# A hybrid decoder layer in float32 on one core: the low halves of the feed-forward weights made by an accumulating DMA

## Chip, core and metric

One core of one Trainium2 chip runs the whole layer in one launch. The metric is the time of one execution on the device in microseconds (us), median of several runs.

## What is computed

One decoder layer on 512 tokens of width 1024, in float32: a first feed-forward, a mixer (a state-space group and differential attention side by side, one projection out), and a second feed-forward. Only the feed-forwards are touched; each is, with d_ff = 2816:

```python
def swiglu(h, w_gate, w_up, w_down):
    return (jax.nn.silu(h @ w_gate) * (h @ w_up)) @ w_down

x = x + 0.5 * swiglu(rms_norm(x, ffn1_norm_w[l]), ffn1_w_gate[l], ffn1_w_up[l], ffn1_w_down[l])
...
x = x + 0.5 * swiglu(rms_norm(x, ffn2_norm_w[l]), ffn2_w_gate[l], ffn2_w_up[l], ffn2_w_down[l])
```

## The kernel before

**Three products for one.** To keep float32's accuracy on TensorE (PE) in its faster float32r type, each operand is split into a high half, its value rounded to float32r, and a low half, the rest. A product is then hi x hi + hi x lo + lo x hi: three matmuls into one bank of PSUM (`mm3`, lines 168 to 172, and `product`, lines 322 to 328).

**Weights come in pieces.** `load_raw` (line 119) loads a piece of up to 128 x 1024 from HBM on SP's queue into one of three `raw` buffers. `split_part` (line 124) makes the halves: the high one by a copy on ScalarE (ACT) into `whi` (at the start of the program and in attention, `pool_hi`, on GpSimd, POOL), the low one by a subtraction on VectorE (DVE) into `wlo`:

```python
    def split_part(raw, hi, lo, a, b):
        if pool_hi[0]:
            G.tensor_scalar(hi[:, a:b], raw[:, a:b], 1.0, 1.0, op0=ALU.mult, op1=ALU.mult)
        else:
            S.copy(hi[:, a:b], raw[:, a:b])
        V.tensor_sub(lo[:, a:b], raw[:, a:b], hi[:, a:b].bitcast(F32))
```

`whi` and `wlo` have four buffers each, which go round: a piece's halves can be written only when PE has read the piece four places before it. The list `pieces` (line 113) holds all pieces of the layer in the order of their use; `prep` (line 139) prepares them in that order, `piece(ahead)` (line 159) hands out the next and prepares one or two further ones.

**A feed-forward** has 22 column tiles for gate and up, in four parts of six or four tiles. Its work is of three kinds (`ffn_plan`, line 73):

- The first part's gate and up take plain pieces of 1024 columns, 24 matmuls of 512 columns each (`std`, line 367; 12 pieces in the first feed-forward, 8 in the second).
- The other parts' gate and up go in pairs of tiles, in a form of Strassen's product with seven block products in place of eight (`seven`, line 330). A *seven* needs two loaded pieces, r1 and r2. Four subtractions on DVE (lines 152 to 155) make a scratch `tw` of two pieces from them. Then there are four splits (line 156), called s0 to s3 here: r1, the first and the second half of `tw`, and half of r2 (512 columns). Each of s0 to s2 serves two block products, s3 one; a block product is 12 matmuls of 256 columns, so a seven is 84. There are 16 sevens in the first feed-forward and 18 in the second.
- The products with w_down (`down`, line 354) take one piece per 128 rows of x: 768 columns (or 512, in parts of four tiles) and three matmuls of 512 columns for each tile. Eight downs of a part run one or two at a time behind the next part's sevens; the last part's eight end the feed-forward. A down ends with an update of x on DVE (line 362).

After the last downs of the first feed-forward, `done1` (line 415) copies x to DRAM on POOL's DMA queue (`xsave`, line 419) and prepares the mixer's operands `xhm`, `xlm` (lines 236, 237) and sums of squares (line 247, on POOL).

**Order.** The program is written in the order above; the framework then sets each engine's order by a list schedule of its own. An engine takes its instructions in its order and stands at one whose semaphores are not there yet.

Of the kernel before, what the change touches and what calls it, by code (L numbers as in the profile page):

```python
# [8 lines left out]
F32 = mybir.dt.float32  # L9
# [4 lines left out]
ALU = mybir.AluOpType  # L14
AX = mybir.AxisListType.X
PSUM = bass.MemoryType.PSUM
DRAM = bass.MemoryType.DRAM

P = 128
T = 512  # L20
# [18 lines left out]
def hymba_layer(ctx: ExitStack, tc: tile.TileContext, xT, gu1, dn1, wxbc, wdt, wz, wv, wqk,  # L39
                wo, gu2, dn2, cols, rows, out):  # L40
    nc = tc.nc
    V, S, G, PE = nc.vector, nc.scalar, nc.gpsimd, nc.tensor
# [4 lines left out]
    psum = {}  # L47

    def psum_open(**bufs):
        """One set of PSUM pools at a time: A tiles take two banks, M and J tiles one."""  # L50
        for cm, _ in reversed(list(psum.values())):
            cm.__exit__(None, None, None)
        psum.clear()
        for tag, n in bufs.items():
            cm = tc.tile_pool(name=f"ps{tag}", bufs=n, space=PSUM)
            psum[tag] = (cm, cm.__enter__())
# [14 lines left out]
        return psum["P"][1].tile([P, T], F32, tag="P", name=name)  # L71

    def ffn_plan(parts, early):
        """Order of the work: a part's products with w_down run between the next part's with gate and up."""
        plan, downs, f = [], [], 0
        for pi, n in enumerate(parts):
            if pi == 0:
                plan += [("std", e, g) for e in range(n) for g in range(2)]
            else:
                for c in range(n):  # L80
                    if pi == 1 and c == 0:
                        plan += downs[:early]
                        downs = downs[early:]
                    plan.append(("seven", f + c // 2 * 2, c % 2))
                    while downs and len(downs) > KD * (n - 1 - c) // n:
                        plan.append(downs.pop(0))
            downs = [("down", pi, d) for d in range(KD)]
            f += n
        return plan + downs
# [23 lines left out]
    pieces = ffn_pieces(gu1, dn1, PARTS1, EARLY1) + [("plain",) + p for p in mixp] + ffn_pieces(gu2, dn2, PARTS2, EARLY2)  # L113
    ready = []
    taken = [0]
    scratch = {}
    pool_hi = [False]

    def load_raw(src, n):
        raw = wpool.tile([P, 1024], F32, tag="raw", name="raw", bufs=3)  # L120
# [3 lines left out]
    def split_part(raw, hi, lo, a, b):  # L124
        if pool_hi[0]:
            G.tensor_scalar(hi[:, a:b], raw[:, a:b], 1.0, 1.0, op0=ALU.mult, op1=ALU.mult)  # L126
        else:
            S.copy(hi[:, a:b], raw[:, a:b])  # L128
        V.tensor_sub(lo[:, a:b], raw[:, a:b], hi[:, a:b].bitcast(F32))  # L129

    def hi_lo():
        return wpool.tile([P, 1024], F32R, tag="whi", name="whi"), wpool.tile([P, 1024], F32R, tag="wlo", name="wlo")
# [41 lines left out]
    xpool_cm = tc.tile_pool(name="x1", bufs=1, side="right")  # L174
    xpool = xpool_cm.__enter__()
    x1 = [xpool.tile([P, T], F32, name=f"x1_{d}") for d in range(KD)]
    # products of zeros while the first loads run: the tensor engine's clock is up when the data comes
    zeros = const.tile([P, T], BF16, name="zeros")
    V.memset(zeros, 0.0)
    warm = pP("warm")  # L180
# [24 lines left out]
    xnpool = xn_cm.__enter__()  # L205

    def rsqrt(dst, v, shape, tag):
        """dst = v ** -0.5 for small tiles: exponent-halving start and Newton steps."""
        y = tiny.tile(shape, F32, tag=f"rs_y{tag}", name="rs_y")
        t = tiny.tile(shape, F32, tag=f"rs_t{tag}", name="rs_t")  # L210
        ti = t.bitcast(I32)
        V.tensor_scalar(ti, v.bitcast(I32), 1, None, op0=ALU.arith_shift_right)
        V.tensor_scalar(y.bitcast(I32), ti, -1, 0x5F3759DF, op0=ALU.mult, op1=ALU.add)
        for it in range(3):
            V.tensor_mul(t, y, y)
            V.scalar_tensor_tensor(t, t, -0.5, v, op0=ALU.mult, op1=ALU.mult)
            V.scalar_tensor_tensor(dst if it == 2 else y, t, 1.5, y, op0=ALU.add, op1=ALU.mult)

    class Normed:
        """x * w in two parts, and the factors 1/rms(x) by token (columns, and a row on all partitions)."""  # L220

        def __init__(self, pool, sqp, wcol, name):
            self.sqp, self.pool = sqp, pool
# [46 lines left out]
    first = []  # L270
# [4 lines left out]
    for d in range(KD):  # L275
# [6 lines left out]
                split_part(first[i], *ready[i], sl.start, sl.stop)  # L282
        n1.square(d, x1[d])
    pool_hi[0] = False
    prep(4)

    def ffn(xn, x, done, name, parts, early):
        """x += 0.5 * swiglu(xn).

        The 128-column tiles of gate and up in the first part take the products as they are. The others take them in  # L290
        pairs, in Winograd's form of Strassen's product of 2x2 blocks (halves of the contraction, of the tokens
        and the two tiles), seven block products in place of eight, on the normalized tokens.
        """
        sp_cm = tc.tile_pool(name=f"str{name}", bufs=1)
        hp_cm = tc.tile_pool(name=f"ffn{name}", bufs=5)
        sp, hp = sp_cm.__enter__(), hp_cm.__enter__()
# [1 line left out]
        al = sp.tile([P, 4, 7, 256], F32R, name=f"al{name}")  # L298

        def operands(i):  # L300
            # 0: A12, 1: A22, 2: S1, 3: S2, 4: S3, 5: S4, 6: A11, 7: A21
            tx = hp.tile([P, 8, 256], F32, tag="hp", name="tx")
            for k, at in ((i, 6), (i + 4, 0)):
                c = xn.wcol + k
                V.scalar_tensor_tensor(tx[:, at:at + 2, :].rearrange("p a b -> p (a b)"), x[k], col[:, c:c + 1],
                                       xn.rbc, op0=ALU.mult, op1=ALU.mult)
            V.tensor_add(tx[:, 2], tx[:, 7], tx[:, 1])
            V.tensor_sub(tx[:, 3], tx[:, 2], tx[:, 6])
            V.tensor_sub(tx[:, 4], tx[:, 6], tx[:, 7])
            V.tensor_sub(tx[:, 5], tx[:, 0], tx[:, 3])  # L310
            S.copy(ah[:, i], tx[:, 0:7])
            V.tensor_sub(al[:, i], tx[:, 0:7], ah[:, i].bitcast(F32))

        def h_pair(g, u):
            """silu(g) * u in two parts; g and u: the two tiles, [P, 2, T]."""
            h = hp.tile([P, 2, 2, T], F32R, tag="hp", name="h")
            S.activation(g, g, AF.Silu)
            V.tensor_mul(u, u, g)
            S.copy(h[:, 0], u)
            V.tensor_sub(h[:, 1], u, h[:, 0].bitcast(F32))  # L320
            return h
# [6 lines left out]
                PE.matmul(ps, lhsT=lo, rhs=ah[:, i, a], start=False, stop=i == 3)  # L328

        def seven(c, u, nm_):  # L330
            """c[:, f, t] = the pair's two tiles by the two halves of the tokens."""
            w = piece(1)
            q = [pP(f"{nm_}{z}") for z in range(4)]
            half = lambda z, b: q[z][:, b * 256:(b + 1) * 256]
            cc = c.rearrange("p f (t b) -> p f t b", t=2)
            c1, u2, u3, u4 = (u[:, z] for z in range(4))
            product(half(0, 0), 6, w[0], 0)
            product(half(0, 1), 0, w[0], 512)
            S.copy(c1, half(0, 0))
            V.tensor_add(cc[:, 0, 0], half(0, 1), c1)  # L340
            product(half(1, 0), 2, w[1], 0)
            product(half(1, 1), 4, w[1], 512)
            product(half(2, 0), 3, w[2], 0)
            V.tensor_add(u2, half(2, 0), c1)
            V.tensor_add(u3, half(1, 1), u2)
            V.tensor_add(cc[:, 1, 1], half(1, 0), u3)
            V.tensor_add(u4, half(1, 0), u2)
            product(half(2, 1), 1, w[2], 512)
            V.scalar_tensor_tensor(cc[:, 0, 1], half(2, 1), -1.0, u3, op0=ALU.mult, op1=ALU.add)
            product(half(3, 0), 5, w[3], 0)  # L350
            V.tensor_add(cc[:, 1, 0], half(3, 0), u4)
# [56 lines left out]
        hp_cm.__exit__(None, None, None)  # L408
        sp_cm.__exit__(None, None, None)

# [1 line left out]
    xsave = dram.tile([KD, P, T], F32, name="xsave")  # L412
    nm = [None]

# [4 lines left out]
        G.dma_start(xsave[d], x1[d])  # L419

    ffn(n1, x1, done1, "1", PARTS1, EARLY1)
    nm = nm[0]
    xpool_cm.__exit__(None, None, None)
    psum_open(A=2, M=2, J=2)

# [1 line left out]
    mix_cm = tc.tile_pool(name="mix", bufs=1)  # L427
    mix = mix_cm.__enter__()
    row = mix.tile([P, NROW], F32, name="row")
# [134 lines left out]
    for n, pair in enumerate(order):  # L564
# [4 lines left out]
        for i in range(2):  # L569
            w = piece()  # L570
# [17 lines left out]
    V.tensor_scalar(e2, nm.v, EPS, None, op0=ALU.mult)  # L588

    def tok_proj(name, cb, ahead=2):  # L590
        """Projection onto 256 columns by token blocks; yields after each block's matmuls."""
        ws = [piece(ahead), piece(ahead)]
        for half in range(2):
            ps = pJ(f"{name}_{half}")
            psv = ps.rearrange("p (b c) -> p b c", c=256)
            for jj in range(2):
                j = half * 2 + jj
                o = psv[:, jj, :]
                for k in range(KD):
                    w = ws[k // 4]  # L600
# [129 lines left out]
            pass  # L730
    last_ssd = lambda: drain_c(8)

# [1 line left out]
    def rsqrt_act(dst, v, shape):  # L734
        """dst = v ** -0.5: exp(-ln(v) / 2) and a Newton step."""
        y = tiny.tile(shape, F32, tag="ra_y", name="ra_y")
        t = tiny.tile(shape, F32, tag="ra_t", name="ra_t")
        S.activation(y, v, AF.Ln)
        S.activation(y, y, AF.Exp, scale=-0.5)
        V.tensor_mul(t, y, y)  # L740
        V.scalar_tensor_tensor(t, t, -0.5, v, op0=ALU.mult, op1=ALU.mult)
        V.scalar_tensor_tensor(dst, t, 1.5, y, op0=ALU.add, op1=ALU.mult)
# [124 lines left out]
        G.tensor_scalar(v, v, -0.5, 1.5, op0=ALU.mult, op1=ALU.add)  # L867
        G.tensor_mul(o, o, v)

    # output projection pieces that fill the tensor engine while the last head's attention runs  # L870
    yhl = []

    def y_split():
# [141 lines left out]
    xn_cm.__exit__(None, None, None)  # L1015
    psum_open(P=8)

# [1 line left out]
    def done2(d):  # L1019
        nc.sync.dma_start(out[d], x2[d])  # L1020

    ffn(n2, x2, done2, "2", PARTS2, EARLY2)


# [59 lines left out]
```

## Times and profile before

| | |
|---|---|
| time, median of 3 runs (lowest to highest) | 1205.1 us (1204.64 to 1206.91) |
| span of the profiled execution, first to last instruction | 1203.1 us, 2.0 us under that median |
| busy: PE, DVE, ACT, POOL | 1163.4, 926.0, 533.8, 210.6 us |
| DMA: loads and stores on SP's queue; POOL's queue | 114.15 MB; 4.20 MB |
| first feed-forward, by its products | 6 to 357 us |
| second, by its products | 854 us to the end |

How to read it: a busy share is an average over stages with different limits, so what a change in one stage is worth is read in a table of that stage's stretches. PE's matmuls overlap in the records (the mean "duration" of one is longer than the distance between two), so the pace is read from the chain of work, which lists the distance. The clock is the share of TensorE's full clock that was granted: 1.00 is 2.4 GHz, 0.50 is 1.2 GHz. The DMA share is the mean busy share of the core's 16 DMA engines.

### The profile page before, as it was taken

The page shows a single profiled execution, that of the slowest core. Times are in us where ns is not written, and L with a number is a line of the kernel's source. Part 1 is how long each engine was busy: PE and PEld are TensorE (multiplying, and loading weights), DVE is VectorE, ACT ScalarE, POOL GpSimd, SP SyncE. Part 2 cuts the span into 40 slices and gives each one's busy share as a digit, 9 for nine tenths or more (in the row PEclk, how much of TensorE's full clock was granted, in tenths as well). Part 3 has the DMA queues.
Part 4 walks back from the last instruction along what each step waited for, and adds up shares of the span by engine and source line. Part 5 has one row for each costly group of instructions (what it writes and reads, how often), then busy time and mean ns, then how long its engine had stood idle before and what let it go on. Part 6 is the DMA issues. An engine that isn't in the chain of part 4 may idle for free.

```text
span 1203.1 us, 19035 instructions
## 1 busy us (share of the span) xinstructions
PE 1163.4 (97%) x7483; PEld 1036.3 (86%) x7483; DVE 926.0 (77%) x1593; ACT 533.8 (44%) x863; POOL 210.6 (18%) x214
## 2 busy tenths in 40 slices
PE   8999999999989999798999998899999999999998
PEld 6889999999967788797998886688789999999997
DVE  6988787787585867989588989636499988787862
ACT  5534343433352355343366675735244443434331
POOL 1000000000031004443255756315100000000000
PEclk9999999999998999899999999999999999999999
DMA  7223333333353224242321102216312333333332
GB/s 231 86 75 97 110 110 97 99 107 88 97 193 114 77 82 140 81 131 73 105 71 36 58 32 76 75 44 209 98 62 89 109 121 100 101 107 102 96 114 83
DMA packets 42393, 119.56 MB, mean 99 GB/s; under 512 B 4608, under 2 KB 9920, under 8 KB 42304
## 3 DMA queue, kind: packets, MB, share of 16 engines
q1 hardware_dynamic: 41024, 114.15, 30.3%
q0 software_dynamic: 1280, 4.20, 1.0%
q8 instruction: 59, 0.97, 0.3%
q14 instruction: 30, 0.25, 0.1%
HBM read 112.00 MB, written 6.32 MB: 98 GB/s over the span
## 4 chain that ended last, share of the span: by engine, by line
PE 40%; DVE 10%; issue 2%; ACT 2%; POOL 1%; DMA 0%; DVEq 0%; ACTq 0%; POOLq 0%
PE s L327 5%; PE s L326 5%; PE s L328 5%; PE dn L170 3%; PE dn L172 3%; PE dn L171 3%; PE wo L170 2%; PE wo L171 2%; PE wo L172 2%; DVE nmx L813 2%; DVE pe L823 1%; PE gu L170 1%; PE gu L172 1%; PE gu L171 1%; DVE wlo L129 1%
## 5 line engine op out<-in xcount | busy, mean ns | idle before, releaser
L129 DVE TENSOR_TENSOR wlo<-raw,whi 128x1024 fp32r<-128x1024 f32 (+3 forms) x225 | 225.9, 1007 | 120.0 <-ACT whi L128 104.4
L128 ACT CAST whi<-raw 128x1024 fp32r<-128x1024 f32 (+2 forms) x204 | 175.7, 865 | 310.2 <-PE s L327 121.7
L327 PE MATMUL s<-al,whi 128*128 128x256 f32 x952 | 265.2, 280 | 0.0
L326 PE MATMUL s<-ah,whi 128*128 128x256 f32 x952 | 263.6, 279 | 0.0
L328 PE MATMUL s<-ah,wlo 128*128 128x256 f32 x952 | 262.6, 279 | 0.0
L327 PEld LDWEIGHTS s<-al,whi 128*128 128x128 f32 x952 | 178.7, 188 | 2.1
L326 PEld LDWEIGHTS s<-ah,whi 128*128 128x128 f32 x952 | 178.5, 188 | 2.0
L328 PEld LDWEIGHTS s<-ah,wlo 128*128 128x128 f32 x952 | 177.2, 187 | 0.1
L170 PE MATMUL dn<-h,whi 128*128 128x512 f32 x352 | 137.6, 394 | 0.0
L172 PE MATMUL dn<-h,wlo 128*128 128x512 f32 x352 | 137.5, 392 | 0.0
L171 PE MATMUL dn<-h,whi 128*128 128x512 f32 x352 | 136.9, 389 | 0.0
L128 ACT CAST whi<-tw 128x1024 fp32r<-128x1024 f32 x68 | 70.3, 1049 | 141.2 <-PE s L327 65.7
L129 DVE TENSOR_TENSOR wlo<-tw,whi 128x1024 fp32r<-128x1024 f32 x68 | 82.1, 1220 | 2.8 <-ACT whi L128 2.5
L172 PEld LDWEIGHTS dn<-h,wlo 128*128 128x128 f32 x352 | 66.1, 188 | 14.6
L171 PEld LDWEIGHTS dn<-h,whi 128*128 128x128 f32 x352 | 66.1, 188 | 12.7
L170 PEld LDWEIGHTS dn<-h,whi 128*128 128x128 f32 x352 | 66.1, 188 | 12.2
L603 PE MATMUL qk<-whi,xhm 128*128 128x256 f32 x256 | 73.3, 287 | 1.1 <-DVE l L820 1.1
L605 PE MATMUL qk<-whi,xlm 128*128 128x256 f32 x256 | 72.8, 285 | 0.0
L604 PE MATMUL qk<-wlo,xhm 128*128 128x256 f32 x256 | 72.7, 284 | 0.0
L362 DVE SCALAR_TENSOR_TENSOR x<-dn,x 128x512 f32<-128x512 f32 x64 | 44.0, 688 | 35.4 <-PE dn L172 34.9
L170 PE MATMUL gu<-xh,whi 128*128 128x512 f32 x160 | 64.9, 406 | 2.7 <-POOL whi L126 1.7
L419 POOL DMA_DIRECT2D xsave<-x x8 | 4.6, 578 | 337.3 <-DVE x L362 337.3
(293 smaller groups left out, 2650.8 us busy)
## 6 DMA issues: line engine op xcount, KB each, us to landing
raw<-in_gu SPq DMA_DIRECT2D x86, 512.0 KB, 3.6
raw<-in_dn SPq DMA_DIRECT2D x48, 384.0 KB, 3.2
raw<-in_wqk SPq DMA_DIRECT2D x16, 512.0 KB, 3.6
raw<-in_wxbc SPq DMA_DIRECT2D x12, 512.0 KB, 3.5
raw<-in_wo SPq DMA_DIRECT2D x10, 512.0 KB, 4.1
raw<-in_dn SPq DMA_DIRECT2D x16, 256.0 KB, 2.7
raw<-in_wz SPq DMA_DIRECT2D x8, 512.0 KB, 3.5
ab<-acs_d SPq DMA_DIRECT2D x8, 512.0 KB, 4.1
```

Source lines behind the costliest of these rows:

```text
L128: S.copy(hi[:, a:b], raw[:, a:b])
L129: V.tensor_sub(lo[:, a:b], raw[:, a:b], hi[:, a:b].bitcast(F32))
L170: PE.matmul(ps, lhsT=hi, rhs=xh, start=start, stop=False)
L171: PE.matmul(ps, lhsT=hi, rhs=xl, start=False, stop=False)
L172: PE.matmul(ps, lhsT=lo, rhs=xh, start=False, stop=stop)
L326: PE.matmul(ps, lhsT=hi, rhs=ah[:, i, a], start=i == 0, stop=False)
L327: PE.matmul(ps, lhsT=hi, rhs=al[:, i, a], start=False, stop=False)
L328: PE.matmul(ps, lhsT=lo, rhs=ah[:, i, a], start=False, stop=i == 3)
L362: V.scalar_tensor_tensor(x[d], ps, 0.5, x[d], op0=ALU.mult, op1=ALU.add)
L603: PE.matmul(o, lhsT=xh, rhs=hi, start=k == 0, stop=False)
L604: PE.matmul(o, lhsT=xh, rhs=lo, start=False, stop=False)
L605: PE.matmul(o, lhsT=xl, rhs=hi, start=False, stop=k == KD - 1)
```

## The change

In both feed-forwards (`dma_lo` is set before their pieces are prepared and cleared after the first) the low half is made in two steps, both given by POOL: POOL writes the negated high half into `wlo`, then a DMA on POOL's queue adds the raw weights onto it, from `raw` or `tw` in SBUF to `wlo` in SBUF. 218 pieces are made so, the first two of the mixer among them; two of the first feed-forward's pieces and two of the second's were prepared before the switch and keep the subtraction. (Comments and docstrings also went; lines move by a few.)

```diff
     pool_hi = [False]
+    dma_lo = [False]
...
             S.copy(hi[:, a:b], raw[:, a:b])
-        V.tensor_sub(lo[:, a:b], raw[:, a:b], hi[:, a:b].bitcast(F32))
+        if dma_lo[0]:
+
+            G.tensor_scalar(lo[:, a:b], hi[:, a:b].bitcast(F32), -1.0, 1.0, op0=ALU.mult, op1=ALU.mult)
+            G.dma_start(lo[:, a:b], raw[:, a:b], accum_op=ALU.add)
+        else:
+            V.tensor_sub(lo[:, a:b], raw[:, a:b], hi[:, a:b].bitcast(F32))
...
     pool_hi[0] = False
+    dma_lo[0] = True
     prep(4)
...
     ffn(n1, x1, done1, "1", PARTS1, EARLY1)
+    dma_lo[0] = False
...
+    dma_lo[0] = True
     ffn(n2, x2, done2, "2", PARTS2, EARLY2)
```

What it does to the engines' orders is shown at two places. The first is POOL in the second feed-forward, one seven and the downs beside it. Before, POOL's list there is empty; it ends with the sums of squares ahead of that feed-forward:

```order
L247 TENSOR_TENSOR acc2_8617<-sq_8710,acc2_8617 128x512
L247 TENSOR_TENSOR acc2_8617<-sq_8734,acc2_8617 128x512
L247 TENSOR_TENSOR acc2_8617<-sq_8758,acc2_8617 128x512
L247 TENSOR_TENSOR acc2_8617<-sq_8825,acc2_8617 128x512
L247 TENSOR_TENSOR acc2_8617<-sq_8892,acc2_8617 128x512
L1079 UNCONDITIONAL_BRANCH
L1079 ISA
```

With the change each piece puts two rows there (L132 is the negation, L133 the accumulating DMA; the 768-column pieces are downs, `raw_10901` and `raw_10903` a seven's r1 and r2):

```order
L132 TENSOR_SCALAR wlo_10897<-whi_10896 128x768
L133 DMA wlo_10897<-raw_10894 128x768
L132 TENSOR_SCALAR wlo_10910<-whi_10909 128x1024
L133 DMA wlo_10910<-raw_10901 128x1024
L132 TENSOR_SCALAR wlo_10915<-whi_10914 128x1024
L133 DMA wlo_10915<-tw2_9019 128x1024
L132 TENSOR_SCALAR wlo_10920<-whi_10919 128x1024
L132 TENSOR_SCALAR wlo_10925<-whi_10924 128x512
L133 DMA wlo_10920<-tw2_9019 128x1024
L133 DMA wlo_10925<-raw_10903 128x512
L132 TENSOR_SCALAR wlo_10952<-whi_10951 128x768
L133 DMA wlo_10952<-raw_10949 128x768
```

The DMA of s2 (`wlo_10920`) stands behind the negation of s3 (`wlo_10925`).

The second place is DVE at the same seven. Before (`raw_10733` and `raw_10735` are r1 and r2 there; `x2_4` and `x2_5` are updated by two downs):

```order
L129 TENSOR_TENSOR wlo_10742<-raw_10733,whi_10741 128x1024
L346 TENSOR_TENSOR cw2_8912<-s21211_10627,cw2_8912 128x256
L347 TENSOR_TENSOR cw2_8912<-s21211_10627,cw2_8912 128x256
L155 TENSOR_TENSOR tw2_8911<-tw2_8911,raw_10733 128x512
L351 TENSOR_TENSOR cw2_8912<-s21213_10629,cw2_8912 128x256
L349 SCALAR_TENSOR_TENSOR cw2_8912<-s21212_10628,cw2_8912 128x256
L362 SCALAR_TENSOR_TENSOR x2_4_8603<-dn2_1_4_10757,x2_4_8603 128x512
L318 TENSOR_TENSOR cw2_8912<-cw2_8912 128x1024
L129 TENSOR_TENSOR wlo_10746<-tw2_8911,whi_10745 128x1024
L129 TENSOR_TENSOR wlo_10750<-tw2_8911,whi_10749 128x1024
L320 TENSOR_TENSOR h_10722<-cw2_8912,h_10722 128x1024
L362 SCALAR_TENSOR_TENSOR x2_5_8604<-dn2_1_5_10783,x2_5_8604 128x512
```

With the change:

```order
L158 TENSOR_TENSOR tw2_9019<-raw_10903,raw_10901 128x512
L159 TENSOR_TENSOR tw2_9019<-raw_10903 128x512
L327 TENSOR_TENSOR h_10889<-cw2_9020,h_10889 128x1024
L160 TENSOR_TENSOR tw2_9019<-raw_10903,tw2_9019 128x512
L369 SCALAR_TENSOR_TENSOR x2_4_8711<-dn2_1_4_10929,x2_4_8711 128x512
L161 TENSOR_TENSOR tw2_9019<-tw2_9019,raw_10901 128x512
L369 SCALAR_TENSOR_TENSOR x2_5_8712<-dn2_1_5_10956,x2_5_8712 128x512
```

The rows into `wlo` are gone from between the updates of x; the four into `tw` stay.

## Rows read from the trace of the kernel before

**Rows 1.** The page: span; busy us, share and instructions by engine.

```profile
span 1203.1 us, 19035 instructions
PE 1163.4 (97%) x7483; PEld 1036.3 (86%) x7483; DVE 926.0 (77%) x1593; ACT 533.8 (44%) x863; POOL 210.6 (18%) x214
```

**Rows 2.** Stretches: length, busy us of PE PEld DVE ACT POOL, clock, DMA share, GB/s.

```profile
120.00:150.00 30.00, 30.00 (x213) 28.08 (x212) 23.56 (x37) 11.50 (x14) 0.00 (x0) 1.00 0.37 110
1110.00:1140.00 30.00, 30.00 (x207) 27.76 (x206) 25.39 (x38) 12.66 (x15) 0.00 (x0) 1.00 0.33 104
```

**Rows 3.** Chain of work, 900 to 960 us: start, us, engine and line.

```profile
901.20 0.47 PE dn L170 x2
...
912.49 0.23 PE s L328 x2
```

**Rows 4.** Groups on DVE, 900 to 1150 us: busy us, mean ns, idle before.

```profile
L129 DVE TENSOR_TENSOR wlo<-tw,whi 128x1024 fp32r<-128x1024 f32 x35 | 42.4, 1220 | 1.3 <-ACT whi L128 1.3
...
L129 DVE TENSOR_TENSOR wlo<-raw,whi 128x512 fp32r<-128x512 f32 x23 | 15.7, 688 | 1.6 <-ACT whi L128 1.2
...
L129 DVE TENSOR_TENSOR wlo<-raw,whi 128x768 fp32r<-128x768 f32 x15 | 14.4, 958 | 18.2 <-ACT whi L128 18.2
L152 DVE TENSOR_TENSOR tw<-raw 128x512 f32<-128x512 f32 x18 | 12.4, 689 | 5.8 <-DMA raw<-in_gu 5.6
```

**Rows 5.** DVE in order of time, end of the first feed-forward: start, us.

```profile
354.60 0.68 DVE L362 SCALAR_TENSOR_TENSOR x<-dn,x 128x512 f32<-128x512 f32 x1
355.20 1.21 DVE L129 TENSOR_TENSOR wlo<-raw,whi 128x1024 fp32r<-128x1024 f32 x1
...
358.02 0.68 DVE L362 SCALAR_TENSOR_TENSOR x<-dn,x 128x512 f32<-128x512 f32 x1
```

**Rows 6.** Waits, 340 to 372 us: who for whom, us, times, longest.

```profile
PE xbc L170 <- DVE x L362: 5.6, 1, 5.6
```

**Rows 7.** Stretches around the first feed-forward's end, columns as in rows 2.

```profile
345.00:348.00 3.00, 3.00 (x14) 2.46 (x14) 3.00 (x4) 2.19 (x5) 1.43 (x2) 1.00 0.97 311
...
362.00:364.00 2.00, 1.75 (x4) 1.50 (x5) 2.00 (x3) 0.72 (x1) 1.57 (x2) 0.50 0.58 229
366.00:368.00 2.00, 2.00 (x7) 1.54 (x6) 0.00 (x0) 0.00 (x0) 0.88 (x4) 0.50 0.06 25
368.00:370.00 2.00, 2.00 (x10) 1.66 (x9) 0.00 (x0) 0.00 (x0) 0.00 (x0) 0.99 0.00 0
```

**Rows 8.** Line 126 on POOL: ns, least, median and most, with its forms.

```profile
L126 POOL TENSOR_SCALAR whi<-raw x21: 399/1048/2004, 4.3 to 704.6; 128x1024 fp32r<-128x1024 f32 x13, 128x256 fp32r<-128x256 f32 x8
```

**Rows 9.** Tile xsave: POOL's issues, 256 KB each, columns as in rows 8.

```profile
L419 POOL DMA_DIRECT2D xsave<-x x8: 539/557/752, 342.1 to 362.4; - x8
```

**Rows 10.** DMA queues, 342 to 366 us, then 810 to 830: packets, MB, share.

```profile
q1 hardware_dynamic: 1128, 3.42, 45.2%
q0 software_dynamic: 640, 2.10, 23.2%
...
q1 hardware_dynamic: 817, 2.48, 39.3%
q0 software_dynamic: 640, 2.10, 30.2%
```

**Rows 11.** Table of stretches, in the second of those, columns as in rows 2.

```profile
822.00:827.00 5.00, 5.00 (x24) 4.14 (x23) 4.69 (x7) 4.83 (x8) 0.70 (x1) 1.00 0.98 361
```

**Rows 12.** DMA issues, median us to landing: whole run; then 810 to 830 us.

```profile
raw<-in_gu SPq DMA_DIRECT2D x86, 512.0 KB, 3.6
...
xsave<-x POOLq DMA_DIRECT2D x8, 256.0 KB, 4.0
...
raw<-in_wo SPq DMA_DIRECT2D x4, 512.0 KB, 5.4
```

**Rows 13.** Groups on ACT, 900 to 1150 us, columns as in rows 4.

```profile
L128 ACT CAST whi<-tw 128x1024 fp32r<-128x1024 f32 x35 | 36.4, 1051 | 72.1 <-PE s L327 25.3 <-PE dn L171 22.5 <-DVE tw L153 8.5
...
L128 ACT CAST whi<-raw 128x512 fp32r<-128x512 f32 x23 | 14.2, 621 | 20.8 <-PE s L327 14.0 <-issue 2.9 <-PE dn L171 1.3
```

## The prediction

> **What bounds the kernel now.** I read the page first. Over the span of 1203.1 us TensorE (PE) is busy for 97% and VectorE (DVE) for 77% [rows 1]. The table of stretches then shows where PE's missing 3% are not: in both feed-forwards PE is busy for 30.00 us of 30, at a granted clock of 1.00 (the 2.4 GHz level), while the DMA engines are busy for 0.33 to 0.37 and GpSimd (POOL) does nothing [rows 2]. The reader is to see there that no PE wait is left in the place where the change works.
>
> The chain gives PE's pace: two 256-column products take 0.23 us, two 512-column ones 0.47 [rows 3]. A *seven* (84 products of 256 columns) so lasts 84 x 0.116 = 9.7 us: its weight buffers s0, s1 and s2 are each read for 2.8 us, s3 for 1.4. A *down* of six tiles (18 products of 512) lasts 18 x 0.23 = 4.1 us, one of four tiles 2.8. The program has 34 sevens, and 48 downs (40 of six tiles, 8 of four) among them: 34 x 9.7 + 40 x 4.1 + 8 x 2.8 = 516 us, or **15.2 us for a seven with its share of downs**. That is the beat a new way of making low halves has to keep. The other products (20 plain gate and up pieces of 5.5 us, and the 16 downs at the ends of the two blocks) have more room and are dealt with last.
>
> **What is removed.** 218 subtractions leave DVE: 1.22 us for 1024 columns, 0.96 for 768, 0.69 for 512 [rows 4]. A beat holds 3 x 1.22 + 0.69 + 1.4 x 0.94 = 5.7 us of them. I cost this at nothing inside the blocks: PE waited for none of it [rows 2]. One place pays. At the end of the first block DVE is behind: it runs a 1.21 us subtraction between two updates of x [rows 5], PE waits 5.6 us for the last update [rows 6], and its clock falls to 0.50 (1.2 GHz) until about 368 us [rows 7]. Without the subtractions up to 5.6 us go, and half of the 6 us at half speed: -8.6 at most. The first mixer piece is now made by POOL too, behind copies to xsave that wait for x; I leave it 3.6 us of that and take **-5 us**.
>
> **What is added, on POOL.** A negation per piece; the nearest row is POOL's own 1024-column tensor_scalar, median 1.05 us, 0.40 for 256 columns [rows 8], so 0.62 for 512 and 0.84 for 768 by the line between. And a DMA issue, 0.56 us [rows 9]. A beat holds 3 x 1.05 + 0.62 + 1.4 x 0.84 + 5.4 x 0.56 = 8.0 us, half of 15.2. With the longest of each row, 2.00 us for a 1024-column negation (the others in proportion) and 0.75 for an issue, it is 13.5: POOL has room either way. Against that speaks a rule of the Trainium skill (SBUF — State Buffer, the "DVE blocks DMA" trap in "SBUF: two separate sides"): POOL can't write its descriptors while VectorE runs certain copies, and a DMA of about 620 ns becomes one of about 3100; by that POOL would need 4.9 + 5.4 x 3.1 = 21.6 us a beat, an estimate from that page, and the time would be some 20 us above my forecast. The trace doesn't agree for the DVE work that stands here: the issues to xsave took 0.54 to 0.75 us [rows 9] in a stretch where DVE was busy for 3.00 us of 3 [rows 7].
>
> **What is added, on the DMA engines.** No row shows an accumulating DMA. Bytes first: 34 x 1.84 MB for the sevens and 17.8 MB for the downs are 80 MB of low halves, 2.36 MB a beat, beside 1.57 MB of loads. Rates: POOL's queue moved 2.10 MB in 23.2% of 24 us, 377 GB/s with SBUF as source, and 348 with SBUF as destination; SP's loads 3.42 MB in 45.2% of 24 us, 315 GB/s [rows 10]. Loads cost 1.57/0.315 = 5.0 us a beat, 0.33 of the beat, as in [rows 2].
> - Lower bound: accumulating costs no more than a copy, 2.36/0.377 = 6.3 us; with loads 11.3, within the beat.
> - Upper bound: each byte occupies an engine three times (source, old destination, result, one after the other): 18.8; with loads 23.8.
> - I take two times (two operands read, the writing overlapped as in a copy): 12.5; with loads **17.5 us against a beat of 15.2**.
>
> No row prices the addition itself. The Trainium skill (Collectives: The Full Stack, "The bandwidth ceiling") measured an adding transfer 1.93 times as dear as a copying one, since it reads two sources; by that the sum would be 12.1 in place of 12.5, and the forecast some 17 us lower. No run here shows it yet.
>
> The engines don't run without gaps: over 20 us with both queues at work they were busy for 0.39 + 0.30 = 0.69, and in its best 5 us for 0.98 [rows 10, 11]. Chained requests (below) are between these; I take the middle, 0.835: 17.5/0.835 = 21.0 us a beat, **5.8 more, and 34 x 5.8 = 197 us**. With 0.98 it is 17.9 (+92), with 0.69 25.4 (+345).
>
> **The chains that keep the queue from being full.** A 256 KB DMA of POOL landed 4.0 us after its issue, a 512 KB load of SP 3.6, or 5.4 beside POOL's traffic [rows 12]. A 512 KB accumulation, by two times, lands after 4.0 + 0.79 MB/0.377 = 6.1 us, by a copy's price after 4.7.
> 1. POOL's order puts s3's negation ahead of s2's DMA in 28 of the 34 sevens (the change's section shows one). s3's buffer is free only when the next seven starts: cast 0.62 [rows 13], negation 0.62, landing 6.1 make 7.3 us, and s2 is due at 5.6: +1.7 a seven (+0.4 by a copy's price).
> 2. A raw buffer is free only when its accumulation has landed. From the start of a seven: 1.3 as above, s3's DMA behind s2's 7.5, the next load 3.6 to 5.4, two tw subtractions 1.4, cast and negation 2.1, landing 6.1: 22.0 to 23.8 us to s1 two sevens on. From there s1, s2, s3 and a down take 11.1. That spans two beats: 16.6 to 17.5 each, against 13.8 with one down: +2.8 to +3.7. Before the change the same chain needed about 10 us a beat.
>
> Each is shorter than 21.0, so they are not added; they are why I don't take 0.98.
>
> The plain pieces: an accumulation 2.8 and a load 1.7 us against 5.5 of PE, no loss; the downs at the ends: 2.2 against 2.8, none. Sum: 1203.1 + 197 - 5 = 1395; the median of the runs stands 2.0 above the profiled span, so **1397 us**. From 0.98 to 0.69 this case gives 1292 to 1545.
>
> **The rivals.**
> - *A copy's price.* The DMA engines then have room, and chain 2 decides: 1.3 + 5.4 + (3.6 to 5.4) + 1.4 + 2.1 + 4.7 + 11.1 over two beats is 14.8 to 15.7, +1.0 to +1.9 a seven, 34 to 65 us: 1234 to 1265. For it: the source is SBUF, not HBM. Against it: two operands.
> - *Three times, or a slow adder.* 23.8 at 0.98 is 24.3 (+309), at 0.835 28.5 (+452): 1509 to 1652. For it: a read, an addition and a write can stand one behind the other. Against it: copies already overlap reading and writing.
> - *The clock.* After the 5.6 us of idle PE ran at 0.50 for some 6 us [rows 7]. If each seven's waits came in one piece of that length, each would cost 3 us more: +102, 1499. Against it: my waits split over s1, s2 and the downs.
> - *Faster.* If an accumulation lands within about 4.3 us of its issue beside the loads, chain 1 has no wait (1.2 + 4.3 = 5.5, under 5.6) and chain 2 fits the beat; then only the end of the first block changes, by up to -8.6: 1196. Against it: 256 KB without an addition took 4.0 [rows 12]; this is twice the bytes.
> - *No change.* Its gains just pay its waits. DVE does lose the work (its list is 218 subtractions shorter), so this is no case of a change that does nothing.
>
> **How the numbers follow.** Chances: forecast 0.48, a copy's price 0.22, three times 0.17, the clock 0.07, faster 0.03, no change 0.03. The range is 1234 to 1600: below it lie faster and no change (0.06), above it about half of the three times (0.09) and little else. About 0.2%, 2.4 us, is what a measurement of this kernel can tell from no change: faster 0.03, same 0.03, slower 0.94.
>
> **What would show it.** Right: in both blocks PE's 30.00 falls to some 22 of 30, its waits end with DMAs into wlo, DMA's share rises to about 0.8, and POOL's queue carries about twice a copy's time per byte (95 MB of results, some 500 us of 16 engines). DVE falls by about 225 us, POOL gains about 300. The wait of 5.6 us at the first block's end is gone. Wrong: wlo DMAs that take a copy's time; PE at 30 of 30; POOL issues of 2 us and more; or waits of PE that end with SP's loads alone.

## The result and the profile after

The changed kernel takes **1394.4 us** (median of 3 runs, 1392.6 to 1399.1) against 1205.1: 1.157 times as long, 95% interval 1.1536 to 1.1603. The prediction was 1397. The profiled execution took 1399.05 us, with a span of 1397.3.

The page of the changed kernel, its parts on the span, the queues, the costliest groups and the DMA issues (the last column is us from issue to landing):

```profile
span 1397.3 us, 19744 instructions
PE 1231.0 (88%) x7483; PEld 1081.2 (77%) x7483; DVE 745.6 (53%) x1375; ACT 531.7 (38%) x863; POOL 618.3 (44%) x650
...
q0 software_dynamic: 32672, 99.11, 37.5%
q1 hardware_dynamic: 41024, 114.15, 26.7%
...
L132 POOL TENSOR_SCALAR wlo<-whi 128x1024 fp32r<-128x1024 f32 (+2 forms) x218 | 240.7, 1124 | 410.8 <-ACT whi L129 368.7
...
L133 POOL DMA_DIRECT2D wlo<-raw x150 | 142.9, 966 | 34.4 <-POOL wlo L132 30.1
...
wlo<-tw POOLq DMA_DIRECT2D x68, 512.0 KB, 6.3
wlo<-raw POOLq DMA_DIRECT2D x52, 512.0 KB, 5.5
...
wlo<-raw POOLq DMA_DIRECT2D x50, 256.0 KB, 6.6
```

Against [rows 1], DVE lost 180 us and POOL gained 408. The queue q0 is POOL's. Its share is 37.5% of 1397.3 us on 16 engines, or 524 us. About 12 us of them are the copies to xsave (4.20 MB), which the kernel before has too, so 94.9 MB of low halves cost 512 us: **185 GB/s**, about half of the 377 of [rows 10]. A 512 KB accumulation from `tw` lands 6.3 us after its issue, one from `raw` 5.5, and one of 256 KB 6.6: in this full queue the landing does not follow the size.

The stretches that answer to [rows 2], and then the stretches that hold the sevens of the two blocks, from the first seven's products to the last (columns: length, busy us of PE, PEld, DVE, ACT, POOL with instruction counts, granted clock, DMA share, GB/s):

```profile
120.00:150.00 30.00, 23.59 (x138) 20.80 (x137) 13.16 (x24) 9.40 (x11) 14.20 (x15) 0.89 0.89 198
1110.00:1140.00 30.00, 25.13 (x159) 23.17 (x158) 13.52 (x24) 9.13 (x11) 13.01 (x14) 0.89 0.91 195
...
83.40:412.20 328.80, 276.30 (x1744) 251.70 (x1743) 119.55 (x212) 98.90 (x120) 160.94 (x174) 0.93 0.88 192
1001.60:1356.80 355.20, 295.28 (x1883) 269.36 (x1882) 139.24 (x239) 105.51 (x130) 173.21 (x188) 0.92 0.87 189
```

The same two stretches of the kernel before:

```profile
77.60:329.80 252.20, 252.20 (x1756) 235.12 (x1755) 196.26 (x297) 97.31 (x118) 0.00 (x0) 1.00 0.33 102
901.00:1165.70 264.70, 264.70 (x1894) 248.80 (x1893) 217.50 (x334) 107.88 (x131) 0.00 (x0) 1.00 0.34 104
```

The sevens took 516.9 us, 15.2 for each of 34, with PE busy throughout; now they take 684.0, **20.1 for each**. The DMA engines work 0.88 x 328.8 + 0.87 x 355.2 = 598 us in them, 17.6 a seven. That is more than the old beat of 15.2, so no ordering of the same transfers could have kept the old time. (The share is not exact: over 2 us it can read 1.05, as below. At 1.05, 16.8 us a seven are still more than 15.2.)

Waits of PE in the changed kernel (engine, tile and line, what it waited for: us in total, times, longest), the five longest that end with a half of a weight piece:

```profile
PE s L335 <- DMA wlo<-tw: 81.2, 31, 4.1
PE s L335 <- DMA wlo<-raw: 14.9, 12, 3.6
PE dn L178 <- DMA wlo<-raw: 13.2, 10, 4.7
PE gu L178 <- DMA wlo<-raw: 5.0, 2, 2.8
...
PE s L333 <- ACT whi L129: 4.1, 5, 1.4
```

Low halves made from tw (s1 and s2) have 81 us of it, all others 33. The 5.6 us for which `xbc` waited for x [rows 6] are down to 0.9. To see where the 194.2 us of span came from, I cut both executions at the first and last products of each part:

| part | before | after | difference |
|---|---|---|---|
| start to the first seven | 77.6 | 83.4 | +5.8 |
| sevens, both blocks | 516.9 | 684.0 | +167.1 |
| downs after the last seven, both blocks | 59.8 | 76.0 | +16.2 |
| end of the first block to the mixer | 6.0 | 1.3 | -4.7 |
| mixer | 492.1 | 502.0 | +9.9 |
| plain gate and up, second block | 46.6 | 46.6 | 0 |

The sevens' 167 us are 112 of idle PE (684.0 - 571.6 busy) and 55 of PE running longer at a lower granted clock. The clock falls behind the longer waits, as here in the changed kernel (stretches, same columns as above):

```profile
1118.00:1120.00 2.00, 0.00 (x0) 0.00 (x0) 1.97 (x5) 1.25 (x2) 1.32 (x1) 1.00 0.69 152
1120.00:1122.00 2.00, 0.47 (x2) 0.47 (x3) 1.20 (x1) 1.67 (x3) 1.70 (x3) 0.60 0.18 35
1122.00:1124.00 2.00, 2.00 (x11) 2.00 (x11) 1.69 (x1) 0.28 (x1) 2.00 (x4) 0.50 1.05 174
```

PE is idle for over 3 us, and when it runs again its clock is at 0.50 (1.2 GHz).

### The profile page after: what moved, and what is told of

It is laid out like the page before. It is cut to its first block, busy times and chain, and to the rows that moved or that the text cites. A ratio compares the mean times of both kernels' runs of the same rounds, so it can differ in the third digit from the quotient of the medians.

```text
span 1397.3 us, 19744 instructions
## 1 busy us (share of the span) xinstructions
PE 1231.0 (88%) x7483; PEld 1081.2 (77%) x7483; DVE 745.6 (53%) x1375; ACT 531.7 (38%) x863; POOL 618.3 (44%) x650
## 3 DMA queue, kind: packets, MB, share of 16 engines
q0 software_dynamic: 32672, 99.11, 37.5%
## 4 chain that ended last, share of the span: by engine, by line
PE 26%; DMA 10%; DVE 8%; issue 5%; POOL 3%; ACT 2%; POOLq 0%; DVEq 0%; ACTq 0%; SPq 0%
DMA wlo<-tw 6%; PE s L335 3%; DMA wlo<-raw 3%; PE s L333 2%; PE s L334 2%; PE wo L178 2%; PE wo L176 2%; DMA raw<-in_gu 2%; PE wo L177 2%; POOL wlo L132 2%; DVE nmx L821 1%; PE dn L176 1%; PE dn L177 1%; PE dn L178 1%; PE gu L176 1%
## 5 line engine op out<-in xcount | busy, mean ns | idle before, releaser
L132 POOL TENSOR_SCALAR wlo<-whi 128x1024 fp32r<-128x1024 f32 (+2 forms) x218 | 240.7, 1124 | 410.8 <-ACT whi L129 368.7
L335 PE MATMUL s<-ah,wlo 128*128 128x256 f32 x952 | 283.5, 305 | 96.2 <-DMA wlo<-tw 81.2
L333 PE MATMUL s<-ah,whi 128*128 128x256 f32 x952 | 281.3, 298 | 7.9 <-ACT whi L129 4.1
L335 PEld LDWEIGHTS s<-ah,wlo 128*128 128x128 f32 x952 | 195.0, 208 | 110.2 <-DMA wlo<-tw 90.3
L334 PE MATMUL s<-al,whi 128*128 128x256 f32 x952 | 279.7, 296 | 0.0
L333 PEld LDWEIGHTS s<-ah,whi 128*128 128x128 f32 x952 | 197.0, 207 | 14.0 <-ACT whi L129 6.4
L334 PEld LDWEIGHTS s<-al,whi 128*128 128x128 f32 x952 | 196.4, 206 | 2.4
L133 POOL DMA_DIRECT2D wlo<-raw x150 | 142.9, 966 | 34.4 <-POOL wlo L132 30.1
L351 DVE TENSOR_TENSOR cw<-s,cw 128x256 f32<-128x256 f32 x34 | 14.4, 424 | 228.4 <-PE s L335 228.4
L135 DVE TENSOR_TENSOR wlo<-raw,whi 128x1024 fp32r<-128x1024 f32 (+3 forms) x75 | 82.4, 1104 | 50.4 <-ACT whi L129 42.4
```

The costliest lines, as they stand in the source:

```text
L132: G.tensor_scalar(lo[:, a:b], hi[:, a:b].bitcast(F32), -1.0, 1.0, op0=ALU.mult, op1=ALU.mult)
L133: G.dma_start(lo[:, a:b], raw[:, a:b], accum_op=ALU.add)
L333: PE.matmul(ps, lhsT=hi, rhs=ah[:, i, a], start=i == 0, stop=False)
L334: PE.matmul(ps, lhsT=hi, rhs=al[:, i, a], start=False, stop=False)
```

## Experiments

Theory A is the prediction's: the DMA engines' time for the accumulations, twice a copy's, sets the beat. The rivals stand in the expectations. Unless a run says otherwise it is one execution, beside executions of the kernel before at 1206.1, 1205.7 (median) and 1207.1 us (median). "Rests" are the two blocks from the first seven's start to the last down, 576.7 us before and 760.0 after (278.7 + 298.0, and 368.3 + 391.7).

**1. The addition taken out.** The DMA copies the raw piece over the negated high half, so the low half holds the raw weight.

```
-            G.dma_start(lo[:, a:b], raw[:, a:b], accum_op=ALU.add)
+            G.dma_start(lo[:, a:b].bitcast(F32), raw[:, a:b])
```

> The adding is taken out: POOL still writes the negated high half, but its DMA then copies the raw weights over it (so the low half holds the raw weights). Bytes written, POOL's instructions and their order of dependence stay. Theory A (an accumulation occupies the DMA engines twice as long as a copy, and that is what fills the beat): the software queue's busy share falls from 37.5% of 1397 us (524 us) to some 270 us, a 512 KB transfer lands in under 5.5 us in place of 6.0 to 6.6, and the time falls to 1234 to 1290 us, where the chain through the raw buffer decides. Rival B (the path from SBUF to SBUF through POOL's queue is that slow with or without an addition): queue time near 520 us, time within 20 us of 1394.

Measured: 1264.9 us; the rests are 629.4. The page (queue, group of issues, landing), then the first block's sevens:

```profile
q0 software_dynamic: 26400, 99.11, 20.1%
...
L133 POOL DMA_DIRECT2D wlo<-raw x150 | 86.4, 576 | 35.4 <-POOL wlo L132 29.4
...
wlo<-tw POOLq DMA_DIRECT2D x68, 512.0 KB, 3.7
...
79.90:347.40 267.50, 252.90 (x1744) 232.57 (x1743) 119.85 (x210) 97.58 (x118) 132.16 (x171) 1.00 0.67 234
```

The same bytes now take 20.1% of 1263.2 us, 254, less 12 for xsave: 242 us, 392 GB/s. The addition makes a transfer **2.1 times** as dear, brings its landing from 3.7 to 6.3 us and the record of POOL's issue from 0.58 to 0.97, and is worth 130 of the 189 us. The edit takes out one thing more: the copy writes to a float32 view of the buffer, the accumulation to its float32r type, and the queue's packets fall from 32672 to 26400. What of the 2.1 is the adding and what the type, no run here parts; "the addition" stands for both. DMA's share in the first block's sevens is 0.67, so the engines are no longer full, and 53 us are still lost in the rests: a copy would not have been free either.

**2. No DMA at all.** POOL still negates; DVE adds.

```
-            G.dma_start(lo[:, a:b], raw[:, a:b], accum_op=ALU.add)
+            V.tensor_add(lo[:, a:b], raw[:, a:b], lo[:, a:b].bitcast(F32))
```

> The DMA is taken out: POOL still negates, and VectorE adds the raw weights to the negated half, so DVE has its 218 instructions back and POOL keeps its 218. Theory A (POOL's negations cost nothing by themselves): 1200 to 1220 us, PE without waits in the feed-forwards. Rival C (POOL's negations and DVE's two-input instructions hinder each other enough to matter: one negation took up to 5.9 us in the changed kernel): 1250 us or more, with PE's waits ending with wlo on DVE.

Measured: 1223.2 us, 3 above A's interval; the rests are 598.3, +21.6. PE's waits, then the additions for s1 and s2 (mean ns behind the busy time):

```profile
PE s L335 <- DVE wlo L133: 6.7, 14, 1.5
PE dn L178 <- DVE wlo L133: 6.0, 7, 1.1
...
L133 DVE TENSOR_TENSOR wlo<-tw,wlo 128x1024 fp32r<-128x1024 f32 x68 | 95.5, 1410 | 8.5 <-POOL wlo L132 8.5
```

A negation on POOL and an addition on DVE in place of a subtraction so cost some 22 us without any DMA. The extra step lengthens the way to each low half; and rival C may have a part in it too, for the addition takes 1.41 us where the subtraction took 1.22 [rows 4]. The run doesn't part the two, and together they do not explain the rest.

**3. Only s1 and s2 by DMA.** s0, s3 and the downs are subtracted by DVE again (`split_part` and `split_w` get a flag).

```
-        if dma_lo[0]:
+        if dma_lo[0] and by_dma:
...
+            ready.append([split_w(r1, 1024), split_w(t[:, :1024], 1024, True), split_w(t[:, 1024:], 1024, True),
```

> Only s1 and s2 of each seven (the two halves of tw, 68 accumulations, 36 MB) go by DMA; s0, s3 and all other pieces are subtracted by VectorE as before. Theory A (throughput of the DMA engines): a beat then needs 1.05 MB at 186 GB/s, 5.7 us, and 5.1 us of loads, 10.8 of 15.2, so the queue empties and the time is 1205 to 1235 us. Rival D (the latency of each accumulation decides, not how many there are): most of PE's waits on wlo from tw, 81 us, stay, and the time is 1280 us or more.

Measured: 1251.5 us, between the two theories. A stretch and the first wait:

```profile
76.20:344.40 268.20, 256.47 (x1757) 236.50 (x1756) 166.80 (x266) 97.61 (x118) 61.83 (x60) 0.99 0.64 157
```

```profile
PE s L335 <- DMA wlo<-tw: 33.4, 30, 3.5
```

The page's queue, and one s1 in order of time (start, us; the first row's cast waited for PE's last read of the buffer):

```profile
q0 software_dynamic: 11072, 39.85, 16.4%
...
166.86 1.05 ACT L129 CAST whi<-tw 128x1024 fp32r<-128x1024 f32 x1 [2.13 <-PE s L334]
168.00 1.04 POOL L132 TENSOR_SCALAR wlo<-whi 128x1024 fp32r<-128x1024 f32 x1 [9.52 <-DVE wlo L135]
169.34 0.87 POOL L133 DMA_DIRECT2D wlo<-tw  x1 [0.30 <-POOL wlo L132]
...
175.90 0.39 PE L335 MATMUL s<-ah,wlo 128*128 128x256 f32 x1 [0.58 <-DMA wlo<-tw]
```

The price has not changed: 16.4% of 1249.6 us, less 12 for xsave, are 193 us for 35.65 MB, 185 GB/s as in the full change, so it is not the full queue that makes an accumulation dear. But with DMA at 0.64, PE still waits 30 times in 34 sevens. So there is a second cost beside the engines' time: the delay from a free buffer to a finished low half. Where one down of six tiles stands between, s1 takes the buffer of the s2 before it, and is due when s3, the down and the next s0 have run, 1.4 + 4.1 + 2.8 = 8.3 us later, while the way above, from the cast to the product, takes 9.0. The prediction had not worked this chain out. That it is what PE waits for in this run is worked out, not tested: a fifth pair of half buffers was tried only in the full change, where it did nothing (experiment 11).

**4. Second block only.** The first block subtracts on DVE.

```
     pool_hi[0] = False
-    dma_lo[0] = True
     prep(4)
```

> The change in the second feed-forward alone. Theory A (each feed-forward pays for itself, and the mixer's 10 us more, 502 in place of 492, come from the other order that the framework's schedule took there): the first feed-forward ends at 357 us and the mixer takes 492 us as before, the second takes 94 us longer: 1298 us, within 8. Rival E (the mixer's 10 us come with the slow feed-forward itself, through clock or late buffers, or the second feed-forward is slow because of what came before it): another sum, off by 10 us or more.

Measured: 1304.8 us. The second block's rest is 394.5 (+96.5), the first's unchanged at 278.7: the two blocks' losses are separate.

**5. s3 by DVE, all else by DMA** (the flag as in experiment 3, true for s0, s1, s2 and all other pieces).

```
-            ready.append([split_w(r1, 1024), split_w(t[:, :1024], 1024), split_w(t[:, 1024:], 1024),
+            ready.append([split_w(r1, 1024, True), split_w(t[:, :1024], 1024, True), split_w(t[:, 1024:], 1024, True),
                           split_w(b22, 512)])
```

> s3 of each seven (half of r2, 34 pieces) is subtracted by VectorE again; all else as in the change. That takes away 9 MB of 80 MB of accumulations among the sevens, the negation that stood ahead of s2's DMA in POOL's order, and the accumulation that held r2's buffer. Theory A (throughput decides): DMA work of a beat falls from 12.7 + 5.1 to 11.3 + 5.1 us, so at the same share of 0.88 a beat lasts 18.6 in place of 20.2 us: some 1340 us. Theory F (the chains decide: order on POOL and the raw buffer): +1.7 to +3.7 us a seven go, 60 to 125 us: 1270 to 1335 us, and PE's waits on wlo from tw nearly vanish.

Measured: 1324.7 us, inside the rival's interval and 15 under A's figure. It removes 8.9 MB of 95 (9%) and gives back 70 us. The first block's sevens:

```profile
82.70:380.80 298.10, 265.02 (x1745) 242.92 (x1743) 131.76 (x228) 99.13 (x120) 135.87 (x144) 0.96 0.89 199
```

DMA's share stays at 0.89 as in the full change, so time fell with the DMA work (550 us for 598 in both blocks' sevens); the waits for s1 and s2 did not vanish (63.4 us for 81.2). Both theories have a part in it, and this run doesn't part them; experiments 6 and 10 take the chains one by one.

**6. s3's negation on DVE, its DMA still on POOL.** POOL's order then has s2's DMA right behind its own negation, so chain 1 is cut.

```
-            G.tensor_scalar(lo[:, a:b], hi[:, a:b].bitcast(F32), -1.0, 1.0, op0=ALU.mult, op1=ALU.mult)
+            (V if dve_neg else G).tensor_scalar(lo[:, a:b], hi[:, a:b].bitcast(F32), -1.0, 1.0, op0=ALU.mult, op1=ALU.mult)
...
-                          split_w(b22, 512)])
+                          split_w(b22, 512, True)])
```

> Only s3's negation moves, from POOL to VectorE; its DMA stays, and all bytes stay. POOL's list then has no s3 negation ahead of s2's DMA. Theory A: time within 15 us of 1394, since the bytes are the same and the DMA engines are busy for 0.88. Theory F (s2's late DMA is a wait of its own, +1.7 us a seven in 28 sevens): 1394 - 48, so 1335 to 1360 us.

Measured: 1385.5 us, 9 under the median and 7 under the fastest of the three runs; as a wait of its own in 28 sevens chain 1 would have been 28 x 1.7 = 48. It does not set the beat.

**7. The waits filled.** 12 products of zeros, 256 columns each, ahead of the products of s1 and of s2, write to PSUM that the next product overwrites. PE so stands idle for less of the time there.

```
+            for z in range(FILL):
+                PE.matmul(half(1, 0), lhsT=zeros[:, :P], rhs=zeros[:, :256], start=True, stop=True)
             product(half(1, 0), 2, w[1], 0)
```

> Ahead of s1's and of s2's products each seven gets 12 matmuls of zeros, 256 columns, bf16, into the bank that the product then starts anew: some 2.6 us of PE work a seven, 87 us in all, and nothing waits for more. Theory A (PE waits for low halves in most sevens, and the DMA engines set the pace): the filling runs inside the waits, the time rises by less than 30 us. Theory G (the granted clock, 0.94 in these stretches, costs time of its own: some 22 us of PE work in each feed-forward run at half speed): with fewer idle stretches the clock rises above 0.97 and the time falls by 10 to 40 us. If PE's own pace decided, it would rise by about 87.

Measured: 1384.2 us, 10 under the median. The first block's sevens:

```profile
83.80:405.70 321.90, 304.27 (x2137) 275.92 (x2136) 119.65 (x212) 98.93 (x120) 159.80 (x174) 0.98 0.91 199
```

The clock rose from 0.93 to 0.98, PE carries 28 us more here, and the time fell by a little. The slow clock's 55 us lie mostly in time that PE would have waited anyway: with most of it gone the time is only about 10 us shorter, net of what the filling itself adds.

**8. The end of the first block alone**: the kernel before, with the DMA for the last 8 downs of the first block and the first two mixer pieces (median of 4 executions).

```
-                ready.append(split_w(load_raw(src, n), n))
+                ready.append(split_w(load_raw(src, n), n, i >= 52))
```

> The kernel before, but with the accumulating DMA for the last eight downs of the first feed-forward (512 columns each) and the first two mixer pieces alone, where VectorE was behind and PE waited 5.6 us for it. Theory A: that wait and the half-speed stretch behind it shrink as in the changed kernel (5.6 to about 1 us), nothing else changes: 1197 to 1202 us. Rival H (the accumulations land too late for downs of 2.8 us, or the mixer's order changes as in the full change, +10 us): 1205 to 1220 us.

Measured: 1215.4 us, ratio 1.0083 (1.0065 to 1.0101). The wait at the block's end did go, 6.0 us to 1.3, but the downs ahead of it took 9.3 longer, and the mixer 6.1. PE's waits:

```profile
PE dn L178 <- DMA wlo<-raw: 4.8, 2, 3.6
PE z L611 <- ACT sz L628: 3.9, 2, 2.6
```

(`z` is the mixer's.) So the one gain that the change has is paid for twice in its own neighbourhood.

**9 to 11. Which buffer holds the queue.** The changed kernel cut after the first feed-forward, whose x goes out (the mixer and the second feed-forward are left out, with the constants and the products of zeros that they or the start need), since the buffers of the mixer leave no room for a fourth raw buffer. First the cut alone, then with four raw buffers, then with five pairs of half buffers.

```
-        raw = wpool.tile([P, 1024], F32, tag="raw", name="raw", bufs=3)
+        raw = wpool.tile([P, 1024], F32, tag="raw", name="raw", bufs=4)
```

```
-        return wpool.tile([P, 1024], F32R, tag="whi", name="whi"), wpool.tile([P, 1024], F32R, tag="wlo", name="wlo")
+        return wpool.tile([P, 1024], F32R, tag="whi", name="whi", bufs=5), wpool.tile([P, 1024], F32R, tag="wlo", name="wlo", bufs=5)
```

> The changed kernel cut off after the first feed-forward, whose x is the output (mixer and second feed-forward are left out, with the constants and the warm-up that only they or the start need). It is the control for the next two. Its stretch from the first to the last seven should be that of the whole changed kernel, 329 us (before the change 252), with a DMA share of 0.88: 289 us of DMA work.

> The cut kernel with four raw buffers in place of three. Theory F1 (a load waits for the accumulation that still reads its raw buffer, and that makes the gaps in the DMA queue): the stretch of the sevens falls towards the 289 us of DMA work, to 295 to 312 us, with a share of 0.94 or more. Theory F2 (the four whi and wlo buffers make the gaps): it stays within 6 us of the control. No theory lets it go under 289.

> The cut kernel with five whi and wlo buffers in place of four. Theory F2 (cast, negation, issue and landing, 9.1 us, don't fit the 8.3 us between the end of the products that last read the buffer and the start of s1): the stretch falls to 295 to 312 us. Theory F1: it stays within 6 us of the control. Theory A for both: the work of the DMA engines, 289 us, is the floor, so neither comes near 252.

Measured: 443.0, **410.4** and 441.0 us. The sevens of the cut (322.0 us, a little less than the 328.8 of the whole kernel), of four raw buffers and of five half buffers, one row from each:

```profile
83.40:405.40 322.00, 275.25 (x1744) 250.22 (x1743) 121.29 (x212) 98.55 (x120) 160.93 (x173) 0.95 0.88 197
```

```profile
79.40:374.80 295.40, 267.26 (x1744) 244.33 (x1743) 120.56 (x210) 97.96 (x118) 157.00 (x172) 0.97 0.94 211
```

```profile
79.20:406.00 326.80, 274.04 (x1751) 247.16 (x1750) 127.80 (x210) 96.02 (x120) 158.38 (x173) 0.96 0.86 195
```

A fourth raw buffer brings DMA's share from 0.88 to 0.94 and takes 27 us off; a fifth pair of half buffers does nothing. So chain 2 is what left the queue short of full. And with it eased the stretch is 295.4 us, still 43 over the 252.2 before: 0.94 x 295.4 = 278 us of DMA work are the floor under it, and even a full queue would not reach the old time (at the 1.05 that the share can read, as above, 265 us).

**12. Two mixer pieces alone**: the kernel before, with the DMA for the first two mixer pieces (median of 4 executions; `i >= 52` of experiment 8 is `i >= 60`).

> The kernel before, but with the low halves of the first two mixer pieces alone made by the accumulating DMA. VectorE so has two subtractions of 1.2 us fewer where PE waited 5.6 us for it. Theory A: the wait falls by up to 2.4 us and the time to 1201 to 1204 us. Rival H (making these two pieces by DMA is what turns the mixer's order over, which then takes 498 to 504 us in place of 492): 1206 to 1215 us.

Measured: 1215.2 us, ratio 1.0065 (1.0047 to 1.0083): 1 MB of 95 loses 8 us. The mixer takes 502.3 us for 492.1. Waits of PE, first of this run, then of the kernel before:

```profile
PE z L611 <- ACT sz L628: 5.6, 2, 5.1
PE xbc L176 <- DVE x L369: 5.4, 1, 5.4
```

```profile
PE z L603 <- ACT sz L620: 1.3, 1, 1.3
```

The mixer is 498 to 504 us in all whole-kernel runs in which these two pieces go by DMA, and 492 to 495 in the three (2, 3 and 4) in which they don't. The order of the mixer's work turns over when they change, but it does so in experiment 2 as well, whose mixer takes 492.1 us: another order alone need not cost anything. Which of its rows costs the 10 us stays open. The wait at the block's end stays too (5.4 us), so its cause is the downs' subtractions on DVE, as [rows 5] had it, not these pieces.

No version of these beat the kernel before. Four raw buffers or five half buffers in the whole kernel weren't tried: there is no room.

## Why the prediction was right

The time was right to 3 us, the cause was right, and part of the closeness is luck: the sevens were put 30 us too high, and the parts that were put at nothing 32 too low.

- **Removed work on DVE is worth nothing in the blocks.** Right: the subtractions' groups fell from 308 us to 82, the 226 that were counted, and no time came back but for the wait at the first block's end: -4.7 for -5. (DVE's busy time counts overlapping rows once, 926 us for groups of 1008 before, 746 for 802 after, and so fell by 180.)
- **The price of an accumulation.** Right: two times a copy's by choice between one and three, 2.1 by experiment 1. The Trainium skill (Collectives: The Full Stack, "The bandwidth ceiling") has 1.93 between a copying and an adding collective; the trace is near it and somewhat above. With loads, 17.5 us of DMA work a beat were predicted and 17.6 measured. Landing: 6.1 predicted, 6.3 measured for `tw`, but that is in part luck: the prediction's sum goes by size, and under load the 256 KB ones land no sooner (6.6; with the queue nearly empty, in experiment 8, 4.5 for 256 KB and 5.6 for 512).
- **How full the queue runs.** This is the term of the sum that was mis-sized: 0.835 was taken as the middle of 0.69 and 0.98, and 0.88 came. A beat is 20.1 us, not 21.0, and the sevens +167, not +197. What holds it below full is chain 2, as the prediction said; experiment 10 shows it (0.94, and 27 us back in one block). Chain 1 does not set the beat (experiment 6).
- **"The downs at the ends ... none", the start and the mixer at nothing.** Wrong, +16.2, +5.8 and +9.9. For the downs and the plain pieces at the start the prediction compared the engines' time with PE's, and not the landing. Low halves come late for the first block's last downs (7.5 us of waits, the other 5.7 of `dn` lie among the sevens) and at the start (5.0 of `gu`). The second block's last downs wait for none. Some 6 us of the 16.2 are no loss of the downs: 12 and 13 products more stand behind the last seven in the new order. The rows are the wait at the first end and the stretches of both ends with the change, then both ends before it:

```profile
PE dn L178 <- DMA wlo<-raw: 7.5, 3, 4.7
...
412.20:451.70 39.50, 31.93 (x131) 24.86 (x129) 18.30 (x27) 16.26 (x25) 22.39 (x29) 0.96 0.83 205
1356.80:1393.30 36.50, 36.37 (x161) 29.44 (x159) 8.32 (x11) 6.81 (x8) 12.88 (x14) 1.00 0.79 194
```

```profile
329.80:356.30 26.50, 26.50 (x119) 21.77 (x118) 22.07 (x33) 15.81 (x25) 7.69 (x10) 1.00 0.57 196
1165.70:1199.00 33.30, 33.30 (x148) 27.40 (x148) 13.37 (x17) 5.98 (x7) 0.00 (x0) 1.00 0.27 91
```

The mixer's part wasn't foreseen in kind: it comes with the two pieces (experiment 12).
- **The clock** was a rival at 0.07, not a term. It does fall, to 0.93 in the sevens, but at a net cost of about 10 us (experiment 7), not 102: the beat is the DMA engines', and a slower PE mostly waits less.
- **POOL.** It had room, as predicted, though it gained 408 us, not 300: the negations took 241 us where the prices of [rows 8] make 197, and the issues' records 205 (0.87 by the median and not 0.56) where 122 were counted; some 38 of these overlap what follows. The Trainium skill's trap (SBUF — State Buffer, "SBUF: two separate sides") of DMAs that become 3100 ns ones beside VectorE doesn't appear in this mix. None of the eight issues of [rows 9] starts in the stretch from 345 to 348 us that the prediction set beside them, but DVE is as busy around four of them (14.00 us of the 14 from 348 to 362). The issues of the changed kernel (least, median and most ns), most of them in stretches with DVE busy for 36 to 39%:

```profile
L133 POOL DMA_DIRECT2D wlo<-raw x150: 852/877/1535, 17.6 to 1385.1; - x150
L133 POOL DMA_DIRECT2D wlo<-tw x68: 839/873/1160, 83.3 to 1345.1; - x68
```

The least of them is already 0.84, and the same issue without the addition took 0.58 on the mean: it is the addition that lengthens the record, not VectorE.

- **A copy's price**, the strongest rival, gave 1234 to 1265, worked out from chain 2. Experiment 1, which is that rival made real, took 1264.9: at the upper end, with 8.8 us in the mixer that the rival did not have. Its sevens took 562.7 us, 1.3 more each, within the rival's +1.0 to +1.9; that chain 2 is what costs them this is not shown. The rival fell by its premise.

## What to carry to other kernels

Before work moves from a busy engine that nobody waits for to a DMA, price the DMA by every operand that it reads, add the loads that are there, and compare with the beat of the engine that sets the pace; here 17.6 us against 15.2 decided it, whatever the order. A DMA that reads a buffer also holds it until it has landed, so the loads behind it come later: count buffers in landings. And price the delay by itself: experiments 1 and 3 lose 45 to 60 us with DMA engines that are a third idle, and experiment 2, with all the negations and no DMA for the low halves, some 20.

## What was not expected of the hardware

- The record of an accumulating issue is longer on POOL, 0.97 us on the mean for 0.58 by a copy of the same shape, but POOL is mostly not held longer: its next row can start before the record ends. Where it follows at once it starts 0.60 us after the issue does (median of 88 such pairs), behind a copy 0.58 (of 66). One such pair of the changed kernel (start, us):

```profile
1206.48 1.18 POOL L133 DMA_DIRECT2D wlo<-raw  x1
...
1207.05 1.47 POOL L132 TENSOR_SCALAR wlo<-whi 128x768 fp32r<-128x768 f32 x1
```

- A negation on POOL takes by the median what [rows 8] has (1.04 us beside 1.05, each over several shapes), but not always. This row of the changed kernel gives least, median and most ns; the longest is over five times the median, and no run here shows why:

```profile
L132 POOL TENSOR_SCALAR wlo<-whi x218: 607/1042/5881, 16.1 to 1384.0; 128x1024 fp32r<-128x1024 f32 x67, 128x768 fp32r<-128x768 f32 x24, 128x512 fp32r<-128x512 f32 x18
```
